# Layer norm by chunks, residual and gate arithmetic on VectorE, and the last token-stationary tile group by group, in a two-layer diffusion step on one core

## The chip, the core and the metric

The kernel runs on one core of a Trainium2 chip. The metric is the device time of one execution in microseconds (us). Three runs of the kernel before gave a median of 2680.48 us (2664.18 to 2681.79).

## What is computed

Two post-norm layers over 256 tokens: 128 context tokens (group 0) and 128 sample tokens (group 1), width 2048, all in float32. Each layer is

```python
shift1, scale1, gate1, shift2, scale2, gate2 = mods          # silu(c) @ w_mod + b_mod
h = modulate(x, shift1, scale1)                               # x * (1 + scale) + shift
q, k, v, hq, hff, hfb, hi, hgt = split_in(h @ w_in_l)
att = rms_norm(attend(q, k, v, sink_l), attn_g_l)
hg, s_f, s_b = hgrn_mixer(hq, hff, hfb, hi, hgt, ...)         # two chunked scans
mix = jnp.concatenate([att, hg], -1) @ w_o_l
x = layer_norm(DEEPNORM_ALPHA * x + gate1 * mix, ln_g_l[0], ln_b_l[0])
ffn = sq_relu_mlp(modulate(x, shift2, scale2), w_up_l, w_down_l)
x = layer_norm(DEEPNORM_ALPHA * x + gate2 * ffn, ln_g_l[1], ln_b_l[1])
```

The MLP is 2048 to 8192 to 2048. The outputs are the tokens of both groups, the new key and value cache, and the final scan states. The modulation vectors differ between the groups, and the weights do not.

## The kernel before

**Weight tiles.** Every weight matrix is streamed from HBM in tiles of 512 x 512 (two `raw` buffers of 128 x 1024). ScalarE (ACT) copies a raw half to `wh` in the PE's fast 32-bit type (L1324), VectorE (DVE) subtracts, `wl` = raw - `wh` (L1325), and activations are split in the same way into `hh` and `hl` (L408, L409). A product then takes three matmuls: activation high with weight high, low with high, high with low. A *T unit* (w_in in part, w_up) yields features on partitions, 48 matmuls of 256 columns a tile (L436, L438, L439). An *N unit* (w_o, w_down, the rest of w_in) yields tokens on partitions, 24 matmuls of 512 columns a tile, 12 for each group of tokens, into one accumulator `acc` a group (L448 to L450). A unit is four tiles (2048 rows).

**Order.** The order of TensorE (PE), DVE and ACT is set by a list scheduler from its own model of costs. Each engine then executes in that order, and an instruction that waits holds up all behind it. GpSimd (POOL) and the SP queue keep the order of the program text. SP issues the loads of weights, POOL those of small things: the gate chunks (`gate_chunk`, L876) and the layer norm's gain and offset, broadcast to 128 partitions (L998, L999). Both go into a ring of two buffers `G`.

**Side work.** Modulation vectors of later stages are made beside the main products: on PE with few columns (L203), or on DVE, `ma += raw * stat` (L266), and then the w_mod tile that L266 reads must have landed.

**Residual and norm.** A finished N unit of w_o goes through `add_gated`: DVE multiplies the accumulator by the gate (L887), the product is added to `Y` (L892: on DVE for the last chunk of 512 features, on POOL for the others) and DVE takes the statistics (L882). After the last unit `ln_head` forms mean and 1/std (L900, L612 to L618) and normalises all eight blocks of 128 x 512 (L909). `ln_mod` then transposes each block on PE (L931) and applies scale and shift, for group 0 by two DVE operations on 128 x 512 (L934, L936), for group 1 by four ACT operations (L940), and splits the result. `ln_out` forms gain and offset for the residual of the next stage on POOL (L1002, L1003). It is done after w_o of layer 0 (called T1 below), between the layers (T2) and after w_o of layer 1 (T3).

**MLP down.** w_down is done in four quarters of its rows; for each of four chunks, a quarter's sum is added to `Z` on DVE (L1236), and in the last quarter the accumulator is multiplied by the gate (L1240) and added (L1241). Ahead of that, `pre_sum` multiplies the earlier quarters by the gate on POOL (L1224) and adds the residual on DVE (L1225). `ln_last` closes layer 1.

Of the kernel before, what the change touches and what calls it, by code (L numbers as in the profile page):

```python
# [18 lines left out]
T = 128  # L19
# [28 lines left out]
class Unit:  # L48
    """One [2048, 512] block of a weight matrix against the tokens of both groups."""
# [12 lines left out]
def tile_hybrid_step(ctx: ExitStack, tc: tile.TileContext, a, o):  # L62
# [50 lines left out]
    # ---- constants and small parameters  # L113
# [28 lines left out]
    K = {}  # L142
# [40 lines left out]
    # ---- modulation vectors  # L183
# [3 lines left out]
    class Mod:  # L187
        """One modulation vector; its four blocks of 512 features lie 32 partitions apart."""
# [18 lines left out]
    class ModQ:  # L207
        """512 features of one modulation vector, its products summed over four parts of the rows."""
# [38 lines left out]
    class ModH:  # L247
        """1024 features of one modulation vector, summed over the rows on the vector engine, over partitions on the PE."""
# [109 lines left out]
    # ---- queue of side work, advanced one stage per weight tile  # L358
# [42 lines left out]
    # ---- activations, transposed and split in two  # L401
# [9 lines left out]
    # ---- weight tiles  # L411
# [4 lines left out]
    def mm_tile(it, between):  # L416
        un, kg = it.unit, it.kg
        hi, lo = un.act(kg)
        wh, wl = it.wh, it.wl
        if un.ps is None:  # L420
            un.ps = [None, None]
        f = kg == un.groups[0]
        e = kg == un.groups[-1]
        for kk in range(2):
            if kk == 1:
                between()
            ks = range(2 * kk, 2 * kk + 2)
            if un.kind == "T":
                for m in range(4):
                    if f and kk == 0 and m % 2 == 0:  # L430
                        un.ps[m // 2] = accp.tile([128, 512], F32, tag="acc", name=nm("acc"))
                    ps = un.ps[m // 2][:, 256 * (m % 2):256 * (m % 2) + 256]
                    for k in ks:
                        w0 = wh[k][:, 128 * m:128 * m + 128]
                        w1 = wl[k][:, 128 * m:128 * m + 128]
                        pe.matmul(ps, lhsT=w0, rhs=hi[:, k], start=f and k == 0 and m % 2 == 0, stop=False,  # L436
                                  skip_group_check=True)
                        pe.matmul(ps, lhsT=w0, rhs=lo[:, k], start=False, stop=False, skip_group_check=True)  # L438
                        pe.matmul(ps, lhsT=w1, rhs=hi[:, k], start=False, stop=e and k == 3 and m % 2 == 1,  # L439
                                  skip_group_check=True)  # L440
            else:
                for g in range(2):
                    if f and kk == 0:
                        un.ps[g] = accp.tile([128, 512], F32, tag="acc", name=nm("acc"))
                    ps = un.ps[g]
                    gs = slice(128 * g, 128 * g + 128)
                    for k in ks:
                        pe.matmul(ps, lhsT=hi[:, k, gs], rhs=wh[k], start=f and k == 0, stop=False)  # L448
                        pe.matmul(ps, lhsT=hi[:, k, gs], rhs=wl[k], start=False, stop=False)  # L449
                        pe.matmul(ps, lhsT=lo[:, k, gs], rhs=wh[k], start=False, stop=e and k == 3)  # L450
# [12 lines left out]
    # ---- attention  # L463
# [35 lines left out]
    def softmax(l, j, banks_, nk, e):  # L499
        """e[t, head, key] = exp(scale * s - m); returns 1 / (sum + exp(K["sink"] - m))."""  # L500
# [108 lines left out]
    def rstd_of(v, n, scale, eps):  # L609
        """(scale * v + eps) ** -0.5, refined by one Newton step."""  # L610
# [39 lines left out]
    # ---- HGRN  # L650
# [216 lines left out]
    # ---- residual, layer norm  # L867
# [16 lines left out]
    def add_gated(key, n, g, ps, gt, first, last):  # L884
        """y += gate * ps (y starts as alpha * residual)."""
# [5 lines left out]
        else:  # L891
            (dve if n == 3 else pool).tensor_tensor(y, y, t, ALU.add)  # L892
# [3 lines left out]
    def ln_stat(key):  # L896
        """Mean and 1 / sqrt(variance + eps) of every token, one column a group."""
# [23 lines left out]

    def ln_mod(key, AB, dst):
        """h = (xhat * g + b) * (1 + scale) + shift, transposed and split."""
        A, B = AB
        for n in range(4):
            hl = new_act("h")
            for g in range(2):
# [5 lines left out]
                if g == 0:  # L933
                    dve.tensor_tensor(v3(t, 4), v3(pt, 4),  # L934
                                      A[:, 4 * n:4 * n + 4, g:g + 1].to_broadcast([128, 4, 128]), ALU.mult)
                    dve.tensor_tensor(v3(t, 4), v3(t, 4),  # L936
                                      B[:, 4 * n:4 * n + 4, g:g + 1].to_broadcast([128, 4, 128]), ALU.add)
                else:
                    for c in range(4):
                        act.activation(t[:, 128 * c:128 * c + 128], pt[:, 128 * c:128 * c + 128], AF.Identity,  # L940
                                       scale=A[:, 4 * n + c, g:g + 1], bias=B[:, 4 * n + c, g:g + 1])
# [51 lines left out]
    def ln_out(key, li, sink_fn):  # L993
        """x = xhat * g + b, off the critical path."""
        tag = "G"
        for n in range(4):
            gt, bt = u(tag), u(tag)
# [66 lines left out]
    def first_h(n):  # L1064
        s1, sh = modT[0, 1, n], modT[0, 0, n]
        hl = new_act("h")
        for g in range(2):
            x = xT[n][g]
            if g == 0:
                dve.tensor_tensor(v3(x, 4), v3(x, 4), s1[:, :, g:g + 1].to_broadcast([128, 4, 128]), ALU.mult)  # L1070
                dve.tensor_tensor(v3(x, 4), v3(x, 4), sh[:, :, g:g + 1].to_broadcast([128, 4, 128]), ALU.add)
            else:
                for c in range(4):
                    xc = x[:, 128 * c:128 * c + 128]
                    act.activation(xc, xc, AF.Identity, scale=s1[:, c, g:g + 1], bias=sh[:, c, g:g + 1])
# [15 lines left out]
    def layer(l):  # L1091
# [106 lines left out]
        put_call(lambda: ln_head(k1))  # L1198
# [65 lines left out]
        if l + 1 < L:  # L1264
            put_call(lambda: ln_head(k2))
# [19 lines left out]
    # ---- emit  # L1285
# [45 lines left out]
    def main_ahead(i, n):  # L1331
        """Index just past the n-th main tile after position i."""
# [151 lines left out]
```

## Time and profile before

| | |
|---|---|
| median of 3 runs | 2680.48 us |
| profiled execution, first to last instruction | 2678.7 us |
| PE busy | 2553.7 us (95%), mean granted clock 0.982 |
| DVE busy | 1862.2 us (70%) |
| ACT busy | 1212.4 us (45%) |
| POOL busy | 226.2 us (8%) |
| DMA | 652.91 MB, 244 GB/s, share 0.8 to 0.9 in layer 0, about 0.6 in the MLP of layer 1 |

"Busy" counts the time in which an engine executes; PE's idle time is therefore what stands between the kernel and its matmuls, and the waits view says for which instruction PE waited. The columns of each view stand with its first group below. The span of the profiled execution lies 1.8 us under the median of the runs.

### The profile page before, as it was taken

Reading aid. Unit: us, or ns where it says so; the run is one execution under the profiler, and the core shown is the slowest. Engines: PE = TensorE matmul, PEld = TensorE weight load, DVE = VectorE, ACT = ScalarE, POOL = GpSimd, SP = SyncE. Lnnn points to the kernel's source line nnn. Section 1 sums busy time; section 2 is a strip of 40 time slices with the busy share of each in tenths; the row PEclk is TensorE's granted clock in tenths of the full one; section 3 lists DMA queues with packets and bytes.
Section 4 is the critical chain, followed back from the end, with each engine's and each line's share of the span. In section 5 each row is a group of like instructions: output and inputs, shape, how many; then the busy total and the mean of one; then the engine's idle time right before and its main releaser. Section 6 shows DMA issues by size and latency. Waiting matters only on the chain.

```text
span 2678.7 us, 41129 instructions
## 1 busy us (share of the span) xinstructions
PE 2553.7 (95%) x16276; PEld 2189.5 (82%) x16276; DVE 1862.2 (70%) x2290; ACT 1212.4 (45%) x1655; POOL 226.2 (8%) x266
## 2 busy tenths in 40 slices
PE   7999999988999999999998999999899999999996
PEld 4787777656988978979876989898798898998985
DVE  3555777658877868787778777787876556566566
ACT  2434554334444534533533656544454444443442
POOL 2000000014100000000014100000330000000002
PEclk9999999999999999999999999999899999999998
DMA  9879878778887878787778656476666666666664
GB/s 325 272 270 316 279 245 273 264 246 322 276 285 268 276 251 298 267 274 249 260 260 275 238 172 228 149 237 200 200 213 221 208 212 229 203 219 211 212 207 141
DMA packets 192369, 652.91 MB, mean 244 GB/s; under 512 B 22752, under 2 KB 25376, under 8 KB 192176
## 3 DMA queue, kind: packets, MB, share of 16 engines
q1 hardware_dynamic: 177680, 614.56, 67.5%
q0 software_dynamic: 11552, 33.04, 4.2%
q8 instruction: 127, 2.08, 0.3%
q10 hardware_dynamic: 2944, 2.69, 0.3%
q14 instruction: 66, 0.54, 0.1%
HBM read 643.32 MB, written 6.88 MB: 243 GB/s over the span
## 4 chain that ended last, share of the span: by engine, by line
PE 60%; issue 24%; DMA 8%; DVE 6%; ACT 2%; POOL 0%; SPq 0%; DVEq 0%; ACTq 0%; POOLq 0%
PE acc L436 9%; PE acc L438 9%; PE acc L439 9%; PE acc L448 9%; PE acc L449 9%; PE acc L450 9%; DMA raw<-in_w_mod_dram 3%; DMA raw<-in_w_in_dram 2%; PE psm L203 2%; DMA raw<-in_w_o_dram 2%; DVE wl L1325 2%; PE pX L777 1%; ACT wh L1324 1%; PE psm L223 1%; DMA out_nsf_dram<-lf 1%
## 5 line engine op out<-in xcount | busy, mean ns | idle before, releaser
L1324 ACT CAST wh<-raw 128x1024 fp32r<-128x1024 f32 x784 | 821.6, 1050 | 1184.6 <-PE acc L450 444.2
L1325 DVE TENSOR_TENSOR wl<-raw,wh 128x1024 fp32r<-128x1024 f32 x784 | 973.2, 1249 | 455.6 <-ACT wh L1324 452.8
L436 PE MATMUL acc<-hh,wh 128*128 128x256 f32 x3072 | 880.0, 287 | 7.2 <-DVE Z L1236 2.6
L439 PE MATMUL acc<-hh,wl 128*128 128x256 f32 x3072 | 873.6, 285 | 13.2 <-DVE wl L1325 13.0
L438 PE MATMUL acc<-hl,wh 128*128 128x256 f32 x3072 | 873.4, 284 | 1.4 <-DVE hl L409 1.4
L436 PEld LDWEIGHTS acc<-hh,wh 128*128 128x128 f32 x3072 | 592.3, 193 | 45.3 <-issue 20.0
L439 PEld LDWEIGHTS acc<-hh,wl 128*128 128x128 f32 x3072 | 592.2, 193 | 15.3 <-DVE wl L1325 15.2
L438 PEld LDWEIGHTS acc<-hl,wh 128*128 128x128 f32 x3072 | 592.5, 193 | 3.0 <-DVE hl L409 2.3
L266 DVE SCALAR_TENSOR_TENSOR ma<-raw,stat,ma 128x1024 f32<-128x1024 f32 x300 | 381.8, 1293 | 136.8 <-DMA raw<-in_w_mod_dram 135.3
L448 PE MATMUL acc<-wh,fh 128*128 128x512 f32 x1024 | 401.3, 392 | 9.4 <-DVE Z L1236 8.0
L449 PE MATMUL acc<-wl,fh 128*128 128x512 f32 x1024 | 399.7, 390 | 1.8 <-DVE wl L1325 1.8
L450 PE MATMUL acc<-wh,fl 128*128 128x512 f32 x1024 | 399.0, 390 | 0.0
L448 PEld LDWEIGHTS acc<-wh,fh 128*128 128x128 f32 x1024 | 192.6, 188 | 60.1 <-DVE Z L1236 9.7
L449 PEld LDWEIGHTS acc<-wl,fh 128*128 128x128 f32 x1024 | 192.7, 188 | 43.0 <-DVE wl L1325 3.8
L450 PEld LDWEIGHTS acc<-wh,fl 128*128 128x128 f32 x1024 | 192.5, 188 | 40.3
L448 PE MATMUL acc<-wh,hh 128*128 128x512 f32 x320 | 131.1, 413 | 3.8 <-ACT hh L408 2.4
L449 PE MATMUL acc<-wl,hh 128*128 128x512 f32 x320 | 129.4, 404 | 2.4 <-DVE wl L1325 2.4
L450 PE MATMUL acc<-wh,hl 128*128 128x512 f32 x320 | 128.7, 403 | 1.6 <-DVE hl L409 1.6
L876 POOL DMA_DIRECT2D G<-gr x48 | 26.2, 546 | 968.0 <-DVE Z L1241 431.4
L203 PE MATMUL psm<-raw,stat 128*2 128x512 f32 x640 | 96.3, 599 | 9.8 <-DMA raw<-in_w_mod_dram 9.1
L448 PE MATMUL acc<-wh,mxh 128*128 128x512 f32 x256 | 103.4, 404 | 0.9 <-ACT mxh L408 0.5
L449 PE MATMUL acc<-wl,mxh 128*128 128x512 f32 x256 | 100.3, 393 | 0.8 <-DVE wl L1325 0.8
(366 smaller groups left out, 2133.0 us busy)
## 6 DMA issues: line engine op xcount, KB each, us to landing
raw<-in_w_mod_dram SPq DMA_DIRECT2D x384, 512.0 KB, 5.5
raw<-in_w_up_dram SPq DMA_DIRECT2D x256, 512.0 KB, 5.7
raw<-in_w_down_dram SPq DMA_DIRECT2D x256, 512.0 KB, 5.0
raw<-in_w_in_dram SPq DMA_DIRECT2D x208, 512.0 KB, 5.6
raw<-in_w_o_dram SPq DMA_DIRECT2D x64, 512.0 KB, 6.3
G<-gr POOLq DMA_DIRECT2D x48, 256.0 KB, 5.2
G<-in_lng_dram POOLq DMA_DIRECT2D x12, 256.0 KB, 5.3
G<-in_lnb_dram POOLq DMA_DIRECT2D x12, 256.0 KB, 6.1
```

Of the source, the lines that this page charges most:

```text
L203: pe.matmul(self.ps[32 * j:32 * j + 2, :], lhsT=stat[:, k, :], rhs=raw[j // 2][:, 512 * (j % 2):512 * (j % 2) + 512], start=k == 0, stop=k ...
L223: pe.matmul(self.ps[32 * j:32 * j + 2, :], lhsT=stat[:, 4 * k + j, :], rhs=raw[j // 2][:, 512 * (j % 2):512 * (j % 2) + 512], start=k == 0 ...
L266: dve.scalar_tensor_tensor(self.acc[g], raw[h], c, self.acc[g], ALU.mult, ALU.add)
L436: pe.matmul(ps, lhsT=w0, rhs=hi[:, k], start=f and k == 0 and m % 2 == 0, stop=False, skip_group_check=True)
L438: pe.matmul(ps, lhsT=w0, rhs=lo[:, k], start=False, stop=False, skip_group_check=True)
L439: pe.matmul(ps, lhsT=w1, rhs=hi[:, k], start=False, stop=e and k == 3 and m % 2 == 1, skip_group_check=True)
L448: pe.matmul(ps, lhsT=hi[:, k, gs], rhs=wh[k], start=f and k == 0, stop=False)
L449: pe.matmul(ps, lhsT=hi[:, k, gs], rhs=wl[k], start=False, stop=False)
L450: pe.matmul(ps, lhsT=lo[:, k, gs], rhs=wh[k], start=False, stop=e and k == 3)
L777: pe.matmul(pX[:, 128 * m + 32 * c:128 * m + 32 * c + 32], lhsT=kd[:, 128 * m:128 * m + 128], rhs=qb[:, 128 * m + 32 * c:128 * m + 32 * c ...
L1324: act.copy(wh, r)
L1325: dve.tensor_tensor(wl, r, wh.bitcast(F32), ALU.subtract)
```

## The change

1. In `mm_tile`, the last tile of an N unit does its 12 matmuls of group 0 first and then the 12 of group 1; before, each half of the tile's rows did 6 of group 0 and 6 of group 1.
2. `ln_head` is gone. `ln_mod` takes the statistics and normalises each chunk just ahead of its transposes, group 1 first.
3. Scale and shift of group 0 is four DVE operations of 128 x 128, each with both scalars (`scale_shift`), in place of two broadcast operations of 128 x 512. The first activation of the program uses it too.
4. 76 operations of 128 x 512 go from POOL to DVE: 12 of L892, 16 of L1224, 48 of L1002 and L1003.
5. `ln_out` steps 24 times ahead of its first load, 6 times after each pair of loads, and 3 times after each group. These steps order POOL's queue.

```diff
+        if un.kind == "N" and e:
+            for g in range(2):
+                if g == 1:
+                    between()
+                n_tile(un, g, range(4), hi, lo, wh, wl, f, e)
+            return
...
-            (dve if n == 3 else pool).tensor_tensor(y, y, t, ALU.add)
+            dve.tensor_tensor(y, y, t, ALU.add)
...
-    def ln_head(key):
-        mr = ln_stat(key)
-        for n in range(4):
-            for g in range(2):
-                y = yt[key, n, g]
-                dve.tensor_scalar(y, y, mr[g][0], mr[g][1], ALU.subtract, ALU.mult)
...
+    def scale_shift(out, src, A, B, g):
+        for c in range(4):
+            o_, s_ = (x[:, 128 * c:128 * c + 128] for x in (out, src))
+            if g == 0:
+                dve.tensor_scalar(o_, s_, A[:, c, g:g + 1], B[:, c, g:g + 1], ALU.mult, ALU.add)
+            else:
+                act.activation(o_, s_, AF.Identity, scale=A[:, c, g:g + 1], bias=B[:, c, g:g + 1])
...
+        mr = ln_stat(key)
         for n in range(4):
             hl = new_act("h")
-            for g in range(2):
+            for g in (1, 0):
+                y = yt[key, n, g]
+                dve.tensor_scalar(y, y, mr[g][0], mr[g][1], ALU.subtract, ALU.mult)
+            for g in (1, 0):
...
     def ln_out(key, li, sink_fn):
+        for _ in range(24):
+            yield
         for n in range(4):
...
+            for _ in range(6):
+                yield
             for g in range(2):
                 y = yt.pop((key, n, g))
-                pool.tensor_tensor(y, y, gt, ALU.mult)
-                pool.tensor_tensor(y, y, bt, ALU.add)
+                dve.tensor_tensor(y, y, gt, ALU.mult)
+                dve.tensor_tensor(y, y, bt, ALU.add)
                 sink_fn(n, g, y)
-            yield
+                for _ in range(3):
+                    yield
...
-                    pool.tensor_tensor(t, t, gch[l, 5, n, g, 0], ALU.mult)
+                    dve.tensor_tensor(t, t, gch[l, 5, n, g, 0], ALU.mult)
```

Lines move by a few: L882, L887, L892, L909, L1002, L1003, L1224, L1225, L1236, L1240, L1241 and L1325 before are L891, L896, L901, L942, L1013, L1014, L1229, L1230, L1241, L1245, L1246 and L1329 of the changed kernel; L934 and L936 are replaced by L929. A number behind a name is the buffer's serial number.

DVE at T3, before: from the normalising of the last chunk on.

```order
L909 TENSOR_SCALAR Y_17436<-Y_17436,s_17887,s_17891 128x512
L909 TENSOR_SCALAR Y_17440<-Y_17440,s_17887,s_17891 128x512
L934 TENSOR_TENSOR ed_17920<-pt_17915,A_17908 128x512
L934 TENSOR_TENSOR ed_17944<-pt_17939,A_17908 128x512
L936 TENSOR_TENSOR ed_17920<-ed_17920,B_17909 128x512
L936 TENSOR_TENSOR ed_17944<-ed_17944,B_17909 128x512
L409 TENSOR_TENSOR hl_17914<-ed_17930,hh_17913 128x4x128
L409 TENSOR_TENSOR hl_17914<-ed_17920,hh_17913 128x4x128
```

The same place now, from the sixth normalising on (five others stand ahead of it).

```order
L942 TENSOR_SCALAR Y_17271<-Y_17271,s_17916,s_17920 128x512
L929 TENSOR_SCALAR ed_17950<-pt_17945,A_17911,B_17912 128x128 x4
L409 TENSOR_TENSOR hl_17930<-ed_17938,hh_17929 128x4x128
L942 TENSOR_SCALAR Y_17464<-Y_17464,s_17916,s_17920 128x512
L409 TENSOR_TENSOR hl_17930<-ed_17950,hh_17929 128x4x128
```

Six of the eight normalisings, not eight, stand ahead of the first scale and shift, and two operations of the second chunk have moved behind the first chunk's split.

DVE some 12 us later in the same stretch, now: the gain and offset of `ln_out`, with the weight splits (L1329) between them. Before, the splits alone stood here.

```order
L1013 TENSOR_TENSOR Y_17026<-Y_17026,G_18821 128x512
L1013 TENSOR_TENSOR Y_17030<-Y_17030,G_18821 128x512
L1329 TENSOR_TENSOR wl_18178<-raw_18049,wh_18177 128x1024
L1014 TENSOR_TENSOR Y_17026<-Y_17026,G_18822 128x512
L1014 TENSOR_TENSOR Y_17030<-Y_17030,G_18822 128x512
L1013 TENSOR_TENSOR Y_17153<-Y_17153,G_19165 128x512
L1329 TENSOR_TENSOR wl_18234<-raw_18051,wh_18233 128x1024
L1013 TENSOR_TENSOR Y_17157<-Y_17157,G_19165 128x512
L1014 TENSOR_TENSOR Y_17153<-Y_17153,G_19166 128x512
L1329 TENSOR_TENSOR wl_18238<-raw_18111,wh_18237 128x1024
```

G_19165 is loaded into the buffer that G_18821 leaves, so its load is issued after the second row, and the sixth row waits for it with the splits queued behind.

DVE at a chunk's end in the first quarter of w_down, layer 0, before and then now. `ma` rows read a w_mod tile, `acc_8734` and `acc_8750` are group 0's accumulator.

```order
L266 SCALAR_TENSOR_TENSOR ma_8033<-raw_8846,stat,ma_8033 128x1024
L266 SCALAR_TENSOR_TENSOR ma_8032<-raw_8856,stat,ma_8032 128x1024
L1236 TENSOR_TENSOR Z_7104<-Z_7104,acc_8734 128x512
L1236 TENSOR_TENSOR Z_7106<-Z_7106,acc_8741 128x512
L1325 TENSOR_TENSOR wl_8895<-raw_8814,wh_8894 128x1024
```

```order
L266 SCALAR_TENSOR_TENSOR ma_8049<-raw_8862,stat,ma_8049 128x1024
L1241 TENSOR_TENSOR Z_7100<-Z_7100,acc_8750 128x512
L266 SCALAR_TENSOR_TENSOR ma_8048<-raw_8872,stat,ma_8048 128x1024
L1241 TENSOR_TENSOR Z_7102<-Z_7102,acc_8757 128x512
L1329 TENSOR_TENSOR wl_8911<-raw_8830,wh_8910 128x1024
```

Group 0's add stands one `ma` row earlier, and group 1's add now has an `ma` row of another w_mod tile between it and group 0's.

## Rows read from the trace of the kernel before

**Rows 1.** The page: the span, and busy time of each engine.

```profile
span 2678.7 us, 41129 instructions
PE 2553.7 (95%) x16276; PEld 2189.5 (82%) x16276; DVE 1862.2 (70%) x2290; ACT 1212.4 (45%) x1655; POOL 226.2 (8%) x266
```

**Rows 2.** Waits of PE: line, releaser, us in total, times, longest.

```profile
PE acc L439 <- DVE wl L1325: 13.0, 8, 3.4
...
PE pI L748 <- DVE e L742: 9.3, 4, 5.0
...
PE acc L448 <- DVE Z L1236: 8.0, 3, 4.0
...
PE pt L931 <- DVE Y L909: 7.8, 1, 7.8
```

**Rows 3.** Timeline, DVE at T3: start, duration, instruction, count, idle time and releaser.

```profile
1919.02 1.28 DVE L887 TENSOR_TENSOR G<-acc,G 128x512 f32<-128x512 f32 x2
...
1922.78 1.16 DVE L1325 TENSOR_TENSOR wl<-raw,wh 128x1024 fp32r<-128x1024 f32 x1
...
1925.61 6.59 DVE L909 TENSOR_SCALAR Y<-Y,s,s 128x512 f32<-128x512 f32 x8
1932.12 1.28 DVE L934 TENSOR_TENSOR ed<-pt,A 128x512 f32<-128x512 f32 x2
...
1934.52 1.88 DVE L409 TENSOR_TENSOR hl<-ed,hh 128x512 fp32r<-128x512 f32 x3
```

**Rows 4.** Timeline, PE at T3: the first matmul of w_up.

```profile
1935.32 0.78 PE L436 MATMUL acc<-hh,wh 128*128 128x256 f32 x2
```

**Rows 5.** Windows, T3: stretch, its length, busy time of each engine, clock, DMA.

```profile
1917.00:1940.00 23.00, 12.32 (x62) 11.32 (x61) 22.28 (x35) 8.85 (x20) 10.40 (x10) 0.63 0.52 174
```

**Rows 6.** The page, costliest groups: busy us, mean ns, idle before and releaser.

```profile
L1325 DVE TENSOR_TENSOR wl<-raw,wh 128x1024 fp32r<-128x1024 f32 x784 | 973.2, 1249 | 455.6 <-ACT wh L1324 452.8
```

**Rows 7.** Timeline, DVE at T1: the eight normalisings.

```profile
626.92 3.74 DVE L909 TENSOR_SCALAR Y<-Y,s,s 128x512 f32<-128x512 f32 x8
```

**Rows 8.** Timeline, PE at T1: the first low matmul of w_up.

```profile
637.97 0.39 PE L438 MATMUL acc<-hl,wh 128*128 128x256 f32 x1 [1.37 <-DVE hl L409]
```

**Rows 9.** Timeline, PE at T2: a w_mod product, and the first low matmul of w_in.

```profile
1430.02 1.87 PE L203 MATMUL psm<-raw,stat 128*2 128x512 f32 x4 [2.80 <-DMA raw<-in_w_mod_dram]
...
1440.24 0.51 PE L450 MATMUL acc<-wh,hl 128*128 128x512 f32 x1 [1.56 <-DVE hl L409]
```

**Rows 10.** Single lines: count, ns min/median/max, first and last start, form.

```profile
L892 DVE TENSOR_TENSOR Y<-Y,G x4: 677/682/684, 621.9 to 1920.8; 128x512 f32<-128x512 f32 x4
...
L909 DVE TENSOR_SCALAR Y<-Y,s,s x16: 538/542/1494, 626.9 to 1930.7; 128x512 f32<-128x512 f32 x16
...
L801 DVE TENSOR_SCALAR ed<-ed,s x16: 251/264/272, 303.7 to 1693.0; 128x96 f32<-128x96 f32 x16
...
L1325 DVE TENSOR_TENSOR wl<-raw,wh x784: 1160/1224/2332, 33.3 to 2647.3; 128x1024 fp32r<-128x1024 f32 x196
```

**Rows 11.** Line L1224 on POOL: what it waited for (us, times).

```profile
  DMA G<-gr: 20.8, 10
```

**Rows 12.** The page, DMA issues on POOL: count, KB each, median us to landing.

```profile
G<-in_lng_dram POOLq DMA_DIRECT2D x12, 256.0 KB, 5.3
```

**Rows 13.** Timeline, DVE at the chunk's end of the last two order fences.

```profile
958.10 3.68 DVE L266 SCALAR_TENSOR_TENSOR ma<-raw,stat,ma 128x1024 f32<-128x1024 f32 x3 [3.24 <-DMA raw<-in_w_mod_dram]
961.69 1.28 DVE L1236 TENSOR_TENSOR Z<-Z,acc 128x512 f32<-128x512 f32 x2
```

**Rows 14.** Timeline, DVE at a later chunk's end, layer 0.

```profile
1032.40 1.28 DVE L1236 TENSOR_TENSOR Z<-Z,acc 128x512 f32<-128x512 f32 x2
1034.45 1.28 DVE L266 SCALAR_TENSOR_TENSOR ma<-raw,stat,ma 128x1024 f32<-128x1024 f32 x1 [0.77 <-DMA raw<-in_w_mod_dram]
```

**Rows 15.** Timeline, DVE after the last matmuls of the program.

```profile
2657.07 0.69 DVE L1240 TENSOR_TENSOR G<-acc,G 128x512 f32<-128x512 f32 x1
...
2659.71 0.26 DVE L900 BATCH_NORM_AGGREGATE s<-bs 128x2 f32<-128x24 f32 x1
```

More of the change, by code (lines that the diff above doesn't have):

```diff
@@ L427, in mm_tile @@
             ks = range(2 * kk, 2 * kk + 2)
[L428 to L441, printed above, removed]
-                for g in range(2):
[L443 to L450, printed above, removed]
@@ new lines, in mm_tile @@
+            if un.kind == "N":
+                for g in range(2):
+                    n_tile(un, g, ks, hi, lo, wh, wl, f, e)
+                continue
+            for m in range(4):
+                if f and kk == 0 and m % 2 == 0:
+                    un.ps[m // 2] = accp.tile([128, 512], F32, tag="acc", name=nm("acc"))
+                ps = un.ps[m // 2][:, 256 * (m % 2):256 * (m % 2) + 256]
+                for k in ks:
+                    w0 = wh[k][:, 128 * m:128 * m + 128]
+                    w1 = wl[k][:, 128 * m:128 * m + 128]
+                    pe.matmul(ps, lhsT=w0, rhs=hi[:, k], start=f and k == 0 and m % 2 == 0, stop=False,
+                              skip_group_check=True)
+                    pe.matmul(ps, lhsT=w0, rhs=lo[:, k], start=False, stop=False, skip_group_check=True)
+                    pe.matmul(ps, lhsT=w1, rhs=hi[:, k], start=False, stop=e and k == 3 and m % 2 == 1,
+                              skip_group_check=True)
@@ new lines, in n_tile @@
+    def n_tile(un, g, ks, hi, lo, wh, wl, f, e):
+        if f and ks[0] == 0:
+            un.ps[g] = accp.tile([128, 512], F32, tag="acc", name=nm("acc"))
+        ps = un.ps[g]
+        gs = slice(128 * g, 128 * g + 128)
+        for k in ks:
+            pe.matmul(ps, lhsT=hi[:, k, gs], rhs=wh[k], start=f and k == 0, stop=False)
+            pe.matmul(ps, lhsT=hi[:, k, gs], rhs=wl[k], start=False, stop=False)
+            pe.matmul(ps, lhsT=lo[:, k, gs], rhs=wh[k], start=False, stop=e and k == 3)
@@ L920, in ln_coef @@
         return A, B
+    def scale_shift(out, src, A, B, g):
[5 more added lines that the diff above has]
+                act.activation(o_, s_, AF.Identity, scale=A[:, c, g:g + 1], bias=B[:, c, g:g + 1])
     def ln_mod(key, AB, dst):
         A, B = AB
+        mr = ln_stat(key)
         for n in range(4):
             hl = new_act("h")
-            for g in range(2):
+            fs = slice(4 * n, 4 * n + 4)
+            for g in (1, 0):
+                y = yt[key, n, g]
+                dve.tensor_scalar(y, y, mr[g][0], mr[g][1], ALU.subtract, ALU.mult)
+            for g in (1, 0):
                 y = yt[key, n, g]
@@ L932, in ln_mod @@
                 t = u("ed")
[L933 to L941, printed above, removed]
+                scale_shift(t, pt, A[:, fs], B[:, fs], g)
                 split_act(hl, (slice(None), slice(0, 4), slice(128 * g, 128 * g + 128)), v3(t, 4))
@@ L993, in ln_out @@
     def ln_out(key, li, sink_fn):
-        tag = "G"
+        for _ in range(24):
+            yield
         for n in range(4):
-            gt, bt = u(tag), u(tag)
+            gt, bt = u("G"), u("G")
             side.dma_start(gt, a["lng"][li:li + 1, 512 * n:512 * n + 512].partition_broadcast(128))
             side.dma_start(bt, a["lnb"][li:li + 1, 512 * n:512 * n + 512].partition_broadcast(128))
+            for _ in range(6):
+                yield
             for g in range(2):
                 y = yt.pop((key, n, g))
-                pool.tensor_tensor(y, y, gt, ALU.mult)
-                pool.tensor_tensor(y, y, bt, ALU.add)
+                dve.tensor_tensor(y, y, gt, ALU.mult)
+                dve.tensor_tensor(y, y, bt, ALU.add)
                 sink_fn(n, g, y)
-            yield
+                for _ in range(3):
+                    yield
     modseq = deque()
@@ L1068, in first_h @@
             x = xT[n][g]
[L1069 to L1075, printed above, removed]
+            scale_shift(x, x, s1, sh, g)
             split_act(hl, (slice(None), slice(0, 4), slice(128 * g, 128 * g + 128)), v3(x, 4))
@@ L1197, in layer @@
         put_call(drain)
-        put_call(lambda: ln_head(k1))
         put_call(lambda: ln_mod(k1, ln_coef(l, 4, 3, 2 * l), h2))
@@ L1264, in layer @@
         if l + 1 < L:
-            put_call(lambda: ln_head(k2))
             put_call(lambda: ln_mod(k2, ln_coef(l + 1, 1, 0, 2 * l + 1), hcur))
```

## The prediction, made before the changed kernel had run

> **What bounds the kernel now.** I read the page first, then PE's waits, then the timelines of DVE and PE at the three boundaries T1, T2 and T3. PE is busy for 2553.7 of 2678.7 us [rows 1], so all that a change to the other engines can give back is part of the remaining 125 us; the number of matmuls stays the same. The waits view names who holds PE up: DVE's weight splits (13.0 us), a scan operation of DVE (9.3), the adds that free accumulators (8.0) and one wait of 7.8 us for the normalising at T3 [rows 2]. What is to be seen there: most waits that this change touches are waits for DVE's order, and DVE is the engine that now gets 76 operations more. The timeline of T3 then shows that wait step by step: gate multiply from 1919.02, one weight split between the statistics at 1922.78, eight normalisings from 1925.61 to 1932.2, scale and shift from 1932.12, the first low split at 1934.52 [rows 3], and the first matmul of w_up at 1935.32 [rows 4].
>
> **The work that moves.** An add on 128x512 takes DVE 0.68 us [rows 10], so 76 of them are 76 x 0.68 = 52 us more on DVE. POOL's work in turn slowed DVE: eight normalisings take 3.74 us at T1 with POOL idle for the most part [rows 7] and 6.59 at T3 [rows 3], where POOL is busy for 10.4 of 23 us [rows 5]. Over all 784 weight splits the mean is 1249 ns [rows 6] against a median of 1224 [rows 10], 784 x 0.025 = 20 us; with the other kinds that overlap POOL I put the whole at 25 to 50 us. So DVE's total hardly changes, and what counts is where its time lies. SP's order of loads does not change; POOL keeps its loads in order and loses the operations between them. The Trainium skill (SBUF — State Buffer, "SBUF: two separate sides") gives the reason: the two engines hold one pair of SBUF ports in turn, and the loser waits for the whole instruction. The two rows of normalising agree with it.
>
> **T3, step by step.** Group by group, group 0's residual and statistics are done while PE is at group 1's matmuls. On group 1's path stay multiply 0.6, add 0.6 and statistics 0.6 (half of a pair, 1.28, each), group 0's aggregate 0.2, one split 1.1, and the last aggregate and small steps, 1.7 from the split's end to 1925.61 [rows 3], together 4.8 from 1919.02: 1/std at about 1924, 1.7 us earlier. Six normalisings at 3.74/8 = 0.47 are 2.8, against 6.59 for eight: 3.8 us less. Then comes the new scale and shift, whose price no row of before shows. Bounds for one of its four, from the rows of the same operation with 96 and 512 columns, 264 and 542 ns: 0.09, the slope of (542-264)/416 = 0.67 ns a column without a fixed cost, and 0.54, as much as for 512 columns; I take 264 + 32 x 0.67 = 285 ns [rows 10], the nearest in size. So 4 x 0.29 = 1.16 (0.4 to 2.2), where the first matmul before stood behind both pairs, 2.4 us [rows 3]; that gain of 1.2 I do not count in full, since the split of group 0 now follows ACT's copy at once. I come to a first matmul at 1930 to 1931, against 1935.32: **-5 us** (bounds -7 and -2). The Trainium skill (Perfetto Trace Analysis, "Optimizing Scalar/DVE Operations") speaks against splitting one operation into four, as each costs about 125 ns ahead of its columns when PSUM is read; by that, with my slope, an estimate is 4 x 0.21 = 0.84 us, and the sum would be 0.3 us lower.
>
> **T1.** The normalisings were not slowed here, so less is won: two normalisings fewer ahead of scale and shift (0.9), and low splits that POOL no longer slows. PE waited for a low split until 637.97 [rows 8]; I put that at 634 to 635. But PE's other waits here are for w_mod tiles. **-3** (-6 to 0).
>
> **T2.** The same, with PE held until 1440.24 by the low split [rows 9], and a floor under it: the w_mod product ahead of the transposes got its tile only at 1430.02 [rows 9], and that does not move. From there, two transposes, scale and shift and splits need about 5 us: **-4** (-6 to 0).
>
> **`ln_out` behind T3.** Sixteen operations and seven weight splits now alternate. G has two buffers, so each next gain is loaded only after the last use of the one before. Landing is 5.3 us in the median [rows 12], and between release and use DVE has one split and two operations, 1.22 + 2 x 0.68 = 2.6 us: it stands still for some 2 to 2.7 us, three times. Work and waits are 16 x 0.68 + 7 x 1.22 + 3 x 2.4 = 27 us for the splits of three and a half tiles, which at the mean pace of 2678.7 us for 392 tiles (784 splits [rows 6]) last 24 us. DVE is about a tile ahead when it begins, which covers the 3: **+1** (0 to +6).
>
> **Gates in w_down.** L1224 on POOL waited 20.8 us for ten gate loads [rows 11], about 2 us each, and nothing was queued behind it but POOL. On DVE the same wait holds the splits. In the MLP of layer 1 DVE is ahead by a tile and a half at a chunk's end; after the wait the fourth half split is ready about when PE needs it. In layer 0 the lead is less. **+2** (0 to +8).
>
> **Accumulators in w_down.** Group 0's accumulator is complete 2.7 us before the tile's end, not 1.36. But what held PE was DVE's order: at 958.10 the `ma` rows had waited 3.24 us for a w_mod tile, and the adds stood behind them until 961.69 [rows 13]. Group 0's add now comes one `ma` (1.2 us) earlier there, so that PE starts earlier, and group 1's add comes behind another `ma`, of a tile that may be late: at 1034.45 such a row waited for its tile with both adds already done [rows 14], and now one add would stand behind it. Over these and their like I get between -1 and +2 us at each and take **0** (-4 to +4).
>
> **End.** After the last matmul, group 1 needs multiply, add, statistics and aggregate without group 0's in between: three steps of 0.6, 1.8 us from 2657.07 to its aggregate, against 2.64 [rows 15]: **-0.8**.
>
> **Elsewhere.** In layer 1's scans `Z` buffers come free only when `ln_out` has stored its blocks, and these are now made by DVE, later and in another order; four scan blocks share one buffer in turn. That can lengthen a place where PE already waits for a scan (5.0 us at the longest [rows 2]) or be hidden by it: **+2** (-2 to +12). Splits elsewhere that POOL no longer slows, and a clock that falls for a shorter time at T3 (0.63 there [rows 5]): **-1** (-4 to 0).
>
> **Sum**: -5 -3 -4 +1 +2 +0 -0.8 +2 -1 = -8.8 us, 2669.9 against 2678.7; the profiled span lies 1.8 us under the median, so 2670 to 2672. I say **2670 us**.
>
> **Rivals.**
> A, *DVE stands still for loads*. A wait for G, which was POOL's alone, holds weight splits and accumulator adds. For it: only two buffers, and POOL had to wait for gates already [rows 11]. Against: DVE has 30% of its time free [rows 1]. It decides when landing exceeds some 6 us, where the tile of lead is used up. The price: three boundaries with three turnovers of 5.3 - 2.6 = 2.7 us, 24 us, and 21 us of gate waits, 45 if nothing covers them; with half covered and half of the gains kept, 2679 + 22 - 6 = 2695, with none covered 2715.
> A', *POOL's own loads are late*. The mechanism would be POOL's issues being held while DVE is busy with forms that need both ports, so that landing grows from 5.3 to some 8 us: nine turnovers and sixteen gates by 2.7 us, half covered, 34 us, less the gains of 12: 2701. The Trainium skill (SBUF — State Buffer, "SBUF: two separate sides") states that descriptors of loads issued by POOL cannot be written in such a time; no row of before separates this from a busy DMA.
> B, *DVE was the bound at every such place*. Then the waits of PE on splits, adds and normalising (13.0 + 8.0 + 7.8 = 29 us [rows 2]) go, with the end and the low splits of T1 and T2 (3 us): 2647.
> C, *nothing arrives*. In layer 0 loads set the pace, and what PE gains is waited for at the next w_mod tile: T1 and T2 give nothing, T3 pays the gates back, 2678 to 2680.
>
> **Chances.** Forecast (2655 to 2678) 0.52, A and A' 0.17 (A' alone 0.05), B 0.20, C 0.11. The range takes in B and the milder half of A: 2642 to 2696. About 1% (27 us) is what this measurement can tell from no change; the three runs of before are 17.6 us apart. Faster by more than that (below 2653.7): 0.22. Slower (above 2707): 0.08. Within: 0.70.
>
> **What will show it.** T3: normalisings of 0.47 us each, first w_up matmul 11 to 12 us after the last gate multiply began, not 16.3. `ln_out`: DVE idle ahead of L1013 for G, 2 to 3 us each, and no wait of PE for L1329 in the 25 us after T3; if PE waits there, A. L1229 with waits for G of about 2 us, and splits behind them. Accumulator waits in layer 0 still for L1241, behind `ma`. The prediction is wrong if PE's waits for DVE grow in sum, or if they shrink by over 25 us; and if scale and shift of 128x128 takes over 0.54 us.

## The result and the profile after

The changed kernel takes 2652.5 us in the median of four runs (2644.3 to 2653.3), against 2679.1 for the kernel before; the ratio is 0.990 (95% interval 0.987 to 0.993). Measured once more beside other kernels it was 0.989 (0.986 to 0.992), 2650.3 against 2680.3. So it is faster by 1%, about 27 us, where 9 were forecast.

The page of the changed kernel, to be read against [rows 1] and [rows 12]: the same matmuls, 27 us less span; DVE is busy to within 0.1 us as long as before, with 108 instructions more, and POOL less than half as long.

```profile
span 2651.4 us, 41148 instructions
PE 2545.5 (96%) x16276; PEld 2184.3 (82%) x16276; DVE 1862.3 (70%) x2398; ACT 1214.0 (46%) x1655; POOL 106.3 (4%) x190
...
G<-in_lng_dram POOLq DMA_DIRECT2D x12, 256.0 KB, 5.2
```

PE's waits in the changed kernel, against [rows 2] (line, releaser, us in total, times, longest). L436, L439, L448, L449, L742, L748 and L931 before are L445, L448, L457, L458, L751, L757 and L947 here:

```profile
PE pt L947 <- DVE Y L942: 8.6, 2, 7.3
PE acc L448 <- DVE wl L1329: 8.2, 10, 2.1
...
PE acc L458 <- DVE wl L1329: 7.0, 7, 1.9
PE pI L757 <- DVE e L751: 7.0, 4, 2.8
...
PE acc L457 <- DVE Z L1241: 2.8, 2, 2.1
...
PE acc L445 <- DVE Z L1241: 1.7, 1, 1.7
```

One more row of before, beside the 13.0 us for splits in [rows 2]:

```profile
PE acc L449 <- DVE wl L1325: 5.0, 7, 1.4
```

The longest split wait went from 3.4 to 2.1 us, the longest wait for a scan (`pI`) from 5.0 to 2.8, the accumulator waits at N units from 8.0 to 2.8. Splits together still hold PE for 15.2 us, against 18.0, and the wait for the first normalising at T3 is still 7.3. Summed over the whole view, PE's waits for DVE went from 64 to 48 us (62 and 41 in the second trace of either kernel).

**Where the time lies.** Both programs issue the same 14016 main matmuls in the same units, so I cut every trace at the same counts of matmuls: at the last one ahead of T1, T2 and T3, and some way behind each. "ln_out as before" is the mean (and range) of the kernel before in two traces and of three experiments below that leave `ln_out` alone. Times in us.

| stage | ln_out as before, 5 traces | changed, 2 traces | ln_out alone on VectorE, with steps | its steps alone | on VectorE without steps |
|---|---|---|---|---|---|
| start to w_o, layer 0 | 622.0 (617.9 to 626.4) | 620.4, 618.1 | 620.8 | 618.1 | 622.6 |
| T1 | 64.9 (64.1 to 67.2) | 61.5, 59.1 | 59.7 | 62.8 | 66.7 |
| MLP of layer 0 | 732.9 (728.1 to 738.1) | 726.5, 725.8 | 736.0 | 735.2 | 730.8 |
| T2 | 32.9 (31.4 to 35.1) | 29.0, 29.7 | 28.7 | 29.6 | 28.7 |
| scans of layer 1 | 187.5 (183.9 to 190.3) | 181.1, 178.6 | 178.8 | 184.4 | 196.1 |
| attention to w_o, layer 1 | 277.2 (276.3 to 278.1) | 277.0, 280.5 | 276.9 | 275.6 | 279.4 |
| T3 | 57.0 (54.4 to 60.4) | 52.8, 53.2 | 52.8 | 56.3 | 53.4 |
| MLP of layer 1 | 681.4 (681.3 to 681.6) | 681.5, 681.3 | 681.3 | 681.8 | 681.3 |
| end | 22.0 (21.7 to 22.1) | 21.6, 21.7 | 22.1 | 22.1 | 22.1 |

T1, the MLP of layer 0, T2 and the scans move by 2 to 6.5 us between two traces of the kernel before (experiment 8), so a single trace says little there.

**T3**, DVE and PE of the changed kernel, against [rows 3] and [rows 4]:

```profile
1897.37 0.68 DVE L896 TENSOR_TENSOR G<-acc,G 128x512 f32<-128x512 f32 x1
...
1902.43 2.83 DVE L942 TENSOR_SCALAR Y<-Y,s,s 128x512 f32<-128x512 f32 x6
1905.17 1.36 DVE L929 TENSOR_SCALAR ed<-pt,A,B 128x128 f32<-128x128 f32 x4
...
1926.85 0.69 DVE L1013 TENSOR_TENSOR Y<-Y,G 128x512 f32<-128x512 f32 x1 [2.59 <-DMA G<-in_lng_dram]
...
1934.65 1.29 DVE L1013 TENSOR_TENSOR Y<-Y,G 128x512 f32<-128x512 f32 x2 [3.04 <-DMA G<-in_lng_dram]
```

```profile
1908.12 0.50 PE L445 MATMUL acc<-hh,wh 128*128 128x256 f32 x2
```

From group 1's gate multiply to the first matmul of w_up it is 10.8 us. Before, 16.3 us passed from the first of both groups' multiplies, of which group 1's is the second. Counted alike in both, from the start of the last matmul of w_o, it is 12.7 us now and 17.2 before. Normalisings take 0.47 us each. Behind them DVE stands still for G, 2.59 and 3.04 us, as forecast. PE waits for no split in the 25 us behind T3; its first such wait, 34 us behind, is 1.1 us in this trace and 1.75 in the second.

The clock, against [rows 5] (stretch, its length, busy time of each engine, granted clock, DMA):

```profile
1890.00:1913.00 23.00, 15.74 (x91) 14.42 (x90) 22.01 (x44) 12.18 (x25) 1.08 (x2) 0.78 0.57 188
```

The granted clock around T3 is 0.78, where it was 0.63. Before, PE had transposes but no main matmul for 17.2 us, and then started the first dozen matmuls of w_up 0.21 us apart, at 1.2 GHz, until 1938.4; from there they came 0.12 us apart, at 2.4 GHz. Now it has none for 12.7 us, and they come 0.12 us apart from the third on. By these spacings the slow dozen cost about 1 us (an estimate).

**Prices.** Shape, count and ns (min/median/max), of the new scale and shift and of the weight splits:

```profile
L929 DVE TENSOR_SCALAR ed<-pt,A,B x48: 399/404/411, 632.7 to 1916.8; 128x128 f32<-128x128 f32 x48
...
L929 DVE TENSOR_SCALAR ed<-ed,mq,mq x4: 339/340/346, 183.2 to 184.0; 128x128 f32<-128x128 f32 x4
...
L1329 DVE TENSOR_TENSOR wl<-raw,wh x784: 1159/1221/1227, 33.0 to 2620.4; 128x1024 fp32r<-128x1024 f32 x196
```

Not one of 784 splits takes over 1.23 us now; before, the longest took 2.33 [rows 10]. The Trainium skill (SBUF — State Buffer, "SBUF: two separate sides") says that a DVE operation with two inputs in SBUF, such as a split, and a POOL operation that reads SBUF exclude each other for the whole instruction. These rows agree: with hardly any POOL arithmetic left, no split is slowed.

**Layer 0, a chunk's end**, DVE and PE, against [rows 13]:

```profile
953.71 2.48 DVE L266 SCALAR_TENSOR_TENSOR ma<-raw,stat,ma 128x1024 f32<-128x1024 f32 x2 [1.88 <-DMA raw<-in_w_mod_dram]
956.11 0.68 DVE L1241 TENSOR_TENSOR Z<-Z,acc 128x512 f32<-128x512 f32 x1
956.70 1.28 DVE L266 SCALAR_TENSOR_TENSOR ma<-raw,stat,ma 128x1024 f32<-128x1024 f32 x1
957.90 0.68 DVE L1241 TENSOR_TENSOR Z<-Z,acc 128x512 f32<-128x512 f32 x1
```

```profile
956.84 0.50 PE L457 MATMUL acc<-wh,fh 128*128 128x512 f32 x1 [2.06 <-DVE Z L1241]
```

The add still stands behind `ma` rows that wait for a w_mod tile, and PE waits 2.06 us for it instead of 4.0.

### The profile page after: what moved, and what is told of

It reads as the page before. It is cut to its first block, busy times and chain, and to the rows that moved or that the text cites. A ratio compares the mean times of both kernels' runs of the same rounds, so it can differ in the third digit from the quotient of the medians.

```text
span 2651.4 us, 41148 instructions
## 1 busy us (share of the span) xinstructions
PE 2545.5 (96%) x16276; PEld 2184.3 (82%) x16276; DVE 1862.3 (70%) x2398; ACT 1214.0 (46%) x1655; POOL 106.3 (4%) x190
## 4 chain that ended last, share of the span: by engine, by line
PE 55%; issue 31%; DMA 7%; DVE 4%; ACT 1%; POOL 0%; SPq 0%; ACTq 0%; POOLq 0%; DVEq 0%
PE acc L457 8%; PE acc L459 8%; PE acc L458 8%; PE acc L445 8%; PE acc L448 8%; PE acc L447 8%; DMA raw<-in_w_in_dram 3%; PE psm L203 2%; DMA raw<-in_w_mod_dram 1%; DVE wl L1329 1%; PE pX L786 1%; DMA raw<-in_w_o_dram 1%; PE psm L223 1%; ACT wh L1328 1%; DMA out_nsf_dram<-lf 1%
## 5 line engine op out<-in xcount | busy, mean ns | idle before, releaser
L1329 DVE TENSOR_TENSOR wl<-raw,wh 128x1024 fp32r<-128x1024 f32 x784 | 952.1, 1221 | 441.0 <-ACT wh L1328 437.8
L445 PE MATMUL acc<-hh,wh 128*128 128x256 f32 x3072 | 878.7, 286 | 4.3 <-DVE Z L1241 1.7
L448 PE MATMUL acc<-hh,wl 128*128 128x256 f32 x3072 | 872.1, 284 | 8.3 <-DVE wl L1329 8.2
L445 PEld LDWEIGHTS acc<-hh,wh 128*128 128x128 f32 x3072 | 591.2, 192 | 41.4 <-issue 24.3
L448 PEld LDWEIGHTS acc<-hh,wl 128*128 128x128 f32 x3072 | 590.9, 192 | 10.9 <-DVE wl L1329 10.9
L457 PE MATMUL acc<-wh,fh 128*128 128x512 f32 x1024 | 400.3, 391 | 5.1 <-DVE Z L1241 2.8
L458 PE MATMUL acc<-wl,fh 128*128 128x512 f32 x1024 | 398.9, 390 | 2.3 <-DVE wl L1329 2.2
L457 PEld LDWEIGHTS acc<-wh,fh 128*128 128x128 f32 x1024 | 192.2, 188 | 55.1 <-issue 7.7
L458 PEld LDWEIGHTS acc<-wl,fh 128*128 128x128 f32 x1024 | 192.3, 188 | 42.9 <-DVE wl L1329 3.6
L457 PE MATMUL acc<-wh,hh 128*128 128x512 f32 x320 | 130.0, 410 | 2.5 <-ACT hh L408 2.1
L458 PE MATMUL acc<-wl,hh 128*128 128x512 f32 x320 | 127.4, 399 | 4.4 <-DVE wl L1329 4.3
L457 PE MATMUL acc<-wh,mxh 128*128 128x512 f32 x256 | 103.5, 405 | 0.4 <-ACT mxh L408 0.4
L458 PE MATMUL acc<-wl,mxh 128*128 128x512 f32 x256 | 100.4, 393 | 0.5 <-DVE wl L1329 0.5
L459 PE MATMUL acc<-wh,mxl 128*128 128x512 f32 x256 | 100.3, 393 | 0.0
```

What stands on the lines that cost most here:

```text
L1329: dve.tensor_tensor(wl, r, wh.bitcast(F32), ALU.subtract)
```

## Experiments

Ratios are to the kernel before, measured beside it on the same chip, with 95% intervals. The kernel before took 2676.0 us beside experiments 1 to 4, 2678.3 beside 5 to 8 and 2680.3 beside 9 to 12, so a time is to be read with its ratio.

**1. Last tile alone.** Part 1 of the change on the kernel before.

```diff
+        if un.kind == "N" and e:
+            for g in range(2):
...
+                n_tile(un, g, range(4), hi, lo, wh, wl, f, e)
+            return
```

> The kernel before with part 1 alone: the last tile of an N unit group by group. Theory 'order of the accumulator adds': the 10 us that the MLP of layer 0 lost in the changed kernel come from group 0's add standing ahead of late w_mod rows, so this part alone gives 8 to 10 us there, nothing at T1, T2 and T3, 0.5 at the end: 2669 to 2671. Rival 'POOL out of the way': these 10 us come from weight splits that POOL no longer slows, so this part alone gives 0 to 2 us: 2677 to 2680.

Measured: 1.001 (0.999 to 1.003), 2681.8 us. The theory with which I began, that the accumulators' order makes the gain, falls: alone it gives nothing that can be told. The accumulator waits in the MLP of layer 0 did fall to 4.6 us in this trace, from 10.6 and 8.8 in two traces of before, and the end to 21.7, but neither shows in the time. (They are as low, 3.7 us, in experiment 3, without this part.) A wait of PE for another scan operation, L732 of before, in the attention of layer 1, fell too: 4.5 and 5.1 us in the two traces of before, 1.1 to 1.4 in the three with the last tile group by group. That stage is no shorter for it (276.3, 277.0 and 280.5 us).

**2. Chunks alone.** Parts 2 and 3: `ln_head` gone, normalising in `ln_mod`, `scale_shift`.

```diff
-        put_call(lambda: ln_head(k1))
...
+            for g in (1, 0):
+                y = yt[key, n, g]
+                dve.tensor_scalar(y, y, mr[g][0], mr[g][1], ALU.subtract, ALU.mult)
```

> The kernel before with parts 2 and 3 alone: normalising by chunks and scale and shift as four operations; all arithmetic of POOL stays there. Theory 'boundaries': 3 to 4 us each at T1, T2 and T3, and nothing in the MLP: about 2668. Rival 'POOL out of the way': at T3 POOL's ln_out slows the normalisings as before (0.8 us each instead of 0.47), so the boundaries give 2 us each at the most: 2673 to 2676.

Measured: 0.9985 (0.997 to 1.000), 2673.1 us: not to be told from no change. T3 is 54.4 us, the shortest of the five traces (the others 55.9 to 60.4), T1 and T2 as before: the rival's size. Its cause does not show: six normalisings at T3 take 2.83 us in this trace, 0.47 each, since POOL's first operation of `ln_out` starts only as the sixth ends.

**3. Vector arithmetic alone.** Parts 4 and 5.

```diff
-            (dve if n == 3 else pool).tensor_tensor(y, y, t, ALU.add)
+            dve.tensor_tensor(y, y, t, ALU.add)
...
-                    pool.tensor_tensor(t, t, gch[l, 5, n, g, 0], ALU.mult)
+                    dve.tensor_tensor(t, t, gch[l, 5, n, g, 0], ALU.mult)
...
-                pool.tensor_tensor(y, y, gt, ALU.mult)
-                pool.tensor_tensor(y, y, bt, ALU.add)
+                dve.tensor_tensor(y, y, gt, ALU.mult)
+                dve.tensor_tensor(y, y, bt, ALU.add)
```

> The kernel before with parts 4 and 5 alone: the 76 operations on VectorE, ln_out with its steps. Theory 'boundaries and adds': the normalisings run at 0.47 us at T3 (3 us) and low splits at T1 and T2 are not slowed (2 us each), the ln_out operations take 1 to 2 us back: 2673 to 2676, MLP of layer 0 unchanged. Rival 'POOL out of the way': most of the 27 us, 2658 to 2664, with the MLP of layer 0 10 us shorter.

Measured: 0.994 (0.992 to 0.996), 2659.1 us: most of the change. But the MLP of layer 0 is not 10 us shorter in it (732.3), so the rival had the size and not the place: T1, T2 and T3 are 61.9, 29.8 and 52.6, and the scans 179.0.

**4. The whole change without the last tile.**

```diff
-        if un.kind == "N" and e:
...
+            else:
+                for g in range(2):
+                    if f and kk == 0:
```

> The changed kernel with part 1 undone: the last tile by halves as before. Theory 'order of the accumulator adds': 8 to 10 us slower than the changed kernel, in the MLP of layer 0: 2661 to 2663. Rival 'POOL out of the way': within 2 us of the changed kernel, 2651 to 2655.

Measured: 0.993 (0.990 to 0.995), 2659.0 us. This lies between the two forecasts. Beside 0.990 for the whole the intervals overlap: the last tile may give some 7 us here, where it gave none alone. Not in the place that the theory named, though: the MLP of layer 0 is 726.4 us in this trace, as in the changed kernel.

**5. `ln_out` alone**, on VectorE, with its steps.

```diff
+        for _ in range(24):
+            yield
...
-                pool.tensor_tensor(y, y, gt, ALU.mult)
-                pool.tensor_tensor(y, y, bt, ALU.add)
+                dve.tensor_tensor(y, y, gt, ALU.mult)
+                dve.tensor_tensor(y, y, bt, ALU.add)
```

> The kernel before with ln_out alone changed: its 48 operations on VectorE and its steps. Theory 'POOL slows VectorE at the boundaries': ln_out is the POOL work that runs beside the normalisings, splits and low halves there, so it carries most of the 17 us that the whole of the arithmetic gave: -11 to -15, 2661 to 2665. Rival 'shorter way of a result' (0.68 instead of 1.3 us for each add and multiply on the way to a statistic or a sum): ln_out is on no such way, -2 to -5, 2671 to 2674.

Measured: 0.993 (0.991 to 0.996), 2657.8 us. That is more than either forecast, and all of experiment 3: 18 of the 27 us.

**6. The steps of `ln_out` alone**, its arithmetic still on POOL.

```diff
+        for _ in range(24):
+            yield
...
                 pool.tensor_tensor(y, y, gt, ALU.mult)
```

> The kernel before with the steps of ln_out alone (24 ahead, 6 behind the loads, 3 behind a group); its 48 operations stay on POOL and run later. Theory 'POOL slows VectorE at the boundaries': the normalisings are undisturbed, 0.47 us each at T3, and splits further on are slowed instead, where VectorE has time: -5 to -10, 2666 to 2671. Rival 'two engines, one pair of ports anywhere': what is not lost at the boundary is lost behind it, 0 to -3, 2673 to 2676.

Measured: 0.998 (0.996 to 1.000), 2671.9 us: about 5 us, hardly clear of none, where the theory had 5 to 10 and the rival 0 to 3. The theory had the steps keep POOL off the normalisings at T3, and they do not; DVE there, in this kernel and then in experiment 5:

```profile
1912.48 6.59 DVE L909 TENSOR_SCALAR Y<-Y,s,s 128x512 f32<-128x512 f32 x8
```

```profile
1907.62 3.74 DVE L909 TENSOR_SCALAR Y<-Y,s,s 128x512 f32<-128x512 f32 x8
```

Eight normalisings at T3 cost 2.85 us more in each trace in which POOL's `ln_out` computes beside them, and with that T3 stays at 56.3.

**7. Adds and pre_sum alone** on VectorE (the first two pieces of the diff of experiment 3).

> The kernel before with the 12 adds of add_gated and the 16 multiplies of pre_sum on VectorE, ln_out as before. Theory 'POOL slows VectorE at the boundaries': these run at no boundary, -1 to -4, 2672 to 2675. Rival 'shorter way of a result': -8 to -12, 2664 to 2668.

Measured: 1.001 (0.999 to 1.003), 2679.1 us: nothing.

**8. The kernel before, once more.**

> The kernel before, unchanged, for a second trace: how far the time of each stage moves from one execution to the next. If the stages of layer 0 repeat within 1 us, the 10 us of its MLP in the changed kernel are the change's; if they move by 3 us or more, single traces tell of sizes above that alone.

One execution: 2674.0 us, span 2672.2. From the first trace of before it differs by -6.5 us in the MLP of layer 0, -3.1 at T1, -1.9 at T2 and +5.0 in the scans, and by 0.3 in the MLP of layer 1. The theory of experiment 1 had rested on a gain of 10 us in layer 0, read from one trace against one; that is hardly above this spread.

**9. `ln_out` on VectorE without steps**: the arithmetic lines of experiment 5 alone.

> The kernel before with the 48 operations of ln_out on VectorE and nothing else, its steps left out. Theory 'POOL slows VectorE at the boundaries': T1, T2 and T3 are as short as with the steps (about 60, 29 and 53 us from the last matmul before to a point well behind), and of the 8 us in the scans of layer 1 the half that late splits made goes, while the wait of 4 to 5 us for a scan operation stays: -12 to -15, 2662 to 2666. Rival 'the steps do it': the order of POOL's queue is what counts, -3 to -6, 2671 to 2674.

Measured: 1.001 (0.999 to 1.003), 2680.8 us. Neither theory: no gain at all. T2 and T3 are short as forecast (28.7, 53.4), but T1 is 66.7 and the scans take 196.1 us. DVE's waits for G in this kernel, then two of them behind T2 and PE's waits that follow:

```profile
DVE Z L1002 <- DMA G<-in_lng_dram: 11.3, 3, 4.4
DVE Y L1002 <- DMA G<-in_lng_dram: 9.0, 4, 4.7
```

```profile
1450.38 1.29 DVE L1002 TENSOR_TENSOR Z<-Z,G 128x512 f32<-128x512 f32 x2 [3.19 <-DMA G<-in_lng_dram]
...
1473.75 1.29 DVE L1002 TENSOR_TENSOR Z<-Z,G 128x512 f32<-128x512 f32 x2 [3.74 <-DMA G<-in_lng_dram]
...
1477.63 1.29 DVE L1003 TENSOR_TENSOR Z<-Z,G 128x512 f32<-128x512 f32 x2 [2.58 <-DMA G<-in_lnb_dram]
```

```profile
1455.13 0.56 PE L449 MATMUL acc<-wl,hh 128*128 128x512 f32 x1 [3.13 <-DVE wl L1325]
...
1480.11 0.58 PE L439 MATMUL acc<-hh,wl 128*128 128x256 f32 x1 [6.30 <-DVE wl L1325]
```

DVE waits for gain and offset, the splits queue behind it, and PE stands for 3.13 and 6.30 us. This is the forecast's rival A, and the steps are what keeps it away: in experiment 5, which differs by the steps alone, the same waits for gain sum to 9.7 us, not 20.3, and those for offset to 0.7, not 6.9.

**10. `ln_out` without its arithmetic** (48 operations left out), on the kernel before.

```diff
-                pool.tensor_tensor(y, y, gt, ALU.mult)
-                pool.tensor_tensor(y, y, bt, ALU.add)
```

> The kernel before with ln_out's 48 operations left out altogether (the residual of the next stage then lacks gain and offset); loads, stores and steps as before. Theory 'VectorE does them for nothing': within 3 us of the kernel that has them on VectorE without steps. Rival 'VectorE pays for what it takes over': 33 us of work on an engine that is busy 70 per cent costs 5 to 10 us, so this kernel is that much faster.

Measured: 0.996 (0.994 to 0.998), 2667.4 us, and its trace has 58.6, 31.0, 184.4 and 53.2 us for T1, T2, the scans and T3. It is 13 us faster than experiment 9, so VectorE did pay there. The kernel with the same work on VectorE and the steps (experiment 5, 0.993) is no slower than this one, and its scans are 5.6 us shorter (178.8), so the price was one of waits rather than of work. One wait of PE shows where the scans differ:

```profile
PE pI L748 <- DVE e L742: 8.7, 5, 5.2
```

That is the kernel before in its second trace. One such wait of 4.2 to 5.2 us, near 1570, stands in each of the seven traces without steps, this kernel's too (4.56), and in none with them; there the longest wait for this operation is 2.8. The kernel with `ln_out` alone:

```profile
PE pI L748 <- DVE e L742: 3.7, 3, 1.4
```

Counting main matmuls ahead of the scan blocks' first products, the third and fourth block of this group stand behind 7761 and 7770 of them in all seven traces without steps, behind 7824 and 7968 in all seven with. The steps hold `ln_out`'s stores back; in the program's allocation the four blocks then take one `Z` buffer in turn, where they have one each in the kernel before. So they start one after another, and the scheduler puts their products later, where the operands are ready. No experiment shares the buffer without the steps, so that the sharing is what moves the products is read from the program.

**11. `ln_out` and chunks together** (experiments 2 and 5).

> The kernel before with ln_out on VectorE with its steps, and the normalising by chunks with scale and shift as four operations; last tile, adds and pre_sum as before. Theory 'ln_out carries all that can be measured': as with ln_out alone, ratio to before 0.992 to 0.995. Rival 'the chunks add their part once POOL is out of the way': ratio 0.988 to 0.991, as the whole change.

Measured: 0.994 (0.992 to 0.996), 2661.7 us. As `ln_out` alone; the theory.

**12. The whole change, once more.**

> The whole change once more, beside the kernel without last tile and adds. Theory 'ln_out carries all that can be measured': ratio 0.992 to 0.995, and the MLP of layer 0 takes 730 to 736 us in its trace, in the range of the kernel before. Rival 'the rest adds its part': 0.988 to 0.991, and the MLP of layer 0 takes 727 us again.

Measured: 0.989 (0.986 to 0.992), 2650.3 us, with 725.8 us in the MLP of layer 0: the rival. The whole is faster than experiment 11 on the same chip: the intervals just meet (0.989, up to 0.992, against 0.994, down to 0.992), but its slowest of six runs (2653.6 us) lies under the fastest of twelve there (2657.8). No experiment gave a kernel faster than the whole change.

## Why the prediction was right, and where its size was off

2670 was forecast, 2652.5 came: inside the range, on the forecast side, and three times the size. It fell below the forecast's own band (2655 to 2678) and inside the range only because the range took in rival B, which did not decide: to that extent it is luck. "Faster by more than 27 us" had a chance of 0.22, and it came. By its steps, with means of the stage table:

| step | forecast | measured |
|---|---|---|
| T1 | -3 (-6 to 0) | -4.6 |
| T2 | -4 (-6 to 0) | -3.5 |
| T3 with `ln_out` behind it | -5 + 1 | -4.0 |
| gates in w_down, layer 1 | up to +2 | 0.0 |
| accumulators and gates, layer 0 | 0 and up to +2 | -6.7 |
| end | -0.8 | -0.4 |
| scans of layer 1 | +2 (-2 to +12) | -7.6 |
| start, and attention of layer 1 | 0 | -2.7 and +1.6, in or near the spread |

**Right**: the boundaries in size, and in the part of their cause that is POOL's. 1/std came 5.1 us after group 1's gate multiply (forecast 4.8), six normalisings took 2.83 us (2.8), DVE's waits for G at T3 were 2.6, 3.0 and 1.0 us (2 to 2.7, three times) and cost PE 1.1 to 1.75 us (forecast 1), and DVE's total stayed the same. PE's waits for DVE shrank by 17 and 21 us, not by the 25 that were named as a sign of being wrong. The shorter clock dip of the last term shows at T3, with the 1 us estimated above.

**Right in number, not in cause**: the order of the work at the boundaries. The forecast counted on 1/std 1.7 us earlier and on two normalisings fewer ahead of scale and shift. Experiment 5 has neither, and its T1, T2 and T3 take 59.7, 28.7 and 52.8 us, no longer than the whole change (60.3, 29.4 and 53.0 in the mean). Chunks alone spare the normalisings POOL's work as well (experiment 2), so the two ways do not add, and that their sum came near the forecast is luck.

**Scale and shift** of 128x128 takes 404 ns, not 285: inside the bounds of 0.09 and 0.54. The four overlap, 0.32 us from start to start, and take 1.36 us, 0.2 more than the 1.16 of the forecast. The operation reads PSUM and has two scalars, and the row it was taken from (L801) reads SBUF and has one; with two, out of SBUF, it takes 340 ns at this size, and the four start 0.26 us apart. The Trainium skill (Perfetto Trace Analysis, "Optimizing Scalar/DVE Operations") gives DVE an overhead of about 60 ns an operation on SBUF and about 125 on PSUM. The difference, some 60 ns here by either measure, agrees with that; the forecast's estimate of 0.21 us by that page is too low all the same.

**Wrong, the step that failed**: "In layer 1's scans `Z` buffers come free only when `ln_out` has stored its blocks ... **+2**". The fact was right, and its sign was not. I took four blocks sharing one buffer for a delay of blocks that PE waits for. The scheduler knows of that sharing: it moves the blocks' products 63 and 198 matmuls later, and the wait of 5.0 us that PE had there, because those products stood too early in its order, goes (experiments 6 and 10). In experiment 5, with `ln_out` off POOL as well, the stage is 8.7 us under the mean; with VectorE alone it is 8.6 over it. With the steps alone it is 3.1 under, at 184.4, which is inside the range of the five traces and not to be told from no change. All six traces with both take 178.6 to 181.1 us, and none without takes less than 183.9. So this term is a joint one: the work must leave POOL and must also be held back.

**Mis-sized**: the MLP of layer 0. Accumulator waits of the kind in [rows 13] fell, to 4.5 and 3.3 us in the two traces of the whole change; they fell to 3.7 in experiment 3 too, whose stage is 732.3. The stage is 725.8 to 726.5 us long only in kernels with vector arithmetic and chunks together (with the last tile undone also, 726.4), and neither alone does it. With three traces of such kernels, and a spread of 10 us in the others, I leave open which pair is at work, and whether the last tile has a share.

**The gates** had cover: DVE stood still ahead of L1229 eleven times, 9.4 us in all, and the MLP of layer 1 did not move by more than 0.3 us in any kernel with that wait:

```profile
DVE Z L1229 <- DMA G<-gr: 9.4, 11, 2.2
...
DVE Y L1013 <- DMA G<-in_lng_dram: 6.6, 3, 3.0
DVE Z L1013 <- DMA G<-in_lng_dram: 2.1, 2, 1.7
```

Against the rivals: A did not decide in the change (its sign, a wait of PE for a split in the 25 us behind T3, did not come), but it is real (experiment 9). Its upper price does not add up: 2679 + 45 - 6 is 2718, not 2715. A' did not show, with gains landing after 5.2 us in the median as against 5.3. B gave the number that came nearest (2647) and not the cause: the waits for the first normalising at T3 and for splits are for the most part still there (7.3 and 15.2 us). C did not come: T1 and T2 gave 4.6 and 3.5 us.

**The end**, DVE of the changed kernel, against [rows 15]:

```profile
2630.91 0.69 DVE L1246 TENSOR_TENSOR Z<-Z,G 128x512 f32<-128x512 f32 x1
2631.64 0.69 DVE L891 BATCH_NORM_STATS2 bs<-Z 128x6 f32<-128x512 f32 x1
2632.36 0.26 DVE L909 BATCH_NORM_AGGREGATE s<-bs 128x2 f32<-128x24 f32 x1
```

Group 0 is out of the way, as forecast, but alone the three operations wait for each other's results: the steps start 0.72 to 0.73 us apart, not 0.6, so from the start of the multiply to that of the aggregate it is 2.2 us and not 1.8, which takes back half of the 0.8.

## What to carry to other kernels

Where an in-order engine takes over work that waits for loads, price the move and the moment together: here the same 48 operations gave 18 us when they were held back by a few steps, and nothing when they were not. Where a scheduler sets the order, a shared buffer is not only a delay; look where it makes the scheduler put the work that waits. And take a second trace of the kernel before ahead of any story on a stage: two traces of one program differed here by 6.5 us in one stage.

## What the runs showed of the hardware

- Eight normalisings of 128x512 on DVE take 3.74 us with no POOL arithmetic beside them and 6.59 beside that of `ln_out`; the longest weight split was 2.82 us in the second trace of before and 1.23 in the changed kernel.
- A DVE operation with two scalars on 128x128 takes 404 ns when it reads PSUM and 340 when it reads SBUF; four in a row from PSUM start 0.32 us apart.
- A dependent DVE operation on 128x512 starts 0.72 us after the one that it needs, an independent one 0.60.
